# Prompt attention of a hybrid decoder layer: GpSimd in one fixed order, merge weights through DRAM in longer runs, two merged-block buffers, the first value loads on another queue

## The chip, the cores and the metric

The kernel runs on one core of a Trainium2 chip, with 16 DMA engines beside its compute engines. The metric is device time in microseconds (us) from one launch. The time before is 2846.34 us, the median of 3 runs (2836.22 to 2849.17).

## The reference, cut to what matters

One decoder layer over a prompt of 2048 tokens and 8 short samples. Of its parts only the prompt attention and the projection behind it matter here. Each of 8 heads (64 wide) attends in three dilated windows, and the three results are merged by their softmax denominators:

```
PATTERNS = ((128, 1), (512, 4), (2048, 16))
...
def combine_patterns(results):
    outs = jnp.stack([o for o, _ in results], axis=0)
    lses = jnp.stack([l for _, l in results], axis=0)
    w = jax.nn.softmax(lses, axis=0)
    return jnp.sum(w[..., None] * outs, axis=0)

def prompt_attn(q, k, v):
    return combine_patterns([dilated_prompt(q, k, v, w, d) for w, d in PATTERNS])
...
    mixed = jnp.concatenate([o_a.reshape(B, T, -1), o_b.reshape(B, T, -1)], axis=-1).astype(x.dtype) @ w_o
```

## The kernel before, in words

The program has three stages: projections and linear attention, then the prompt attention (`attention`), then the output projection and the feed-forward net (`tail`). The feed-forward net takes more than half of the span and is not touched.

**Attention.** Heads are worked on in four pairs (`pr` 0 to 3). A pair has three patterns (`pat`) of four groups (`g`) each: groups 0 to 3, 4 to 7 and 8 to 11. A group of patterns 0 and 1 has two units of work, one of pattern 2 has one, so a pair has 20 units. A unit (`AtUnit`) is: scores on TensorE (`pas`, L1787), mask and row minimum on VectorE and the exponential on ScalarE, transposes of the result on TensorE (`pat`, L1813), and products with the values (`pao`, L1830). The units are staggered: a unit's transposes come two units after its scores, its products three. TensorE's order over the units is fixed by hand (`AtUnit.line` chains each instruction to the one ahead of it).

**Gathers.** Patterns 1 and 2 need the queries regrouped. `at_gather` has GpSimd copy one tile per head (`aqg`, L1118), two per group, called at the first unit of the group two ahead. There are five such tiles, which is two and a half groups.

**Merge.** When a pair's last unit has been drained, which is three units into the next pair, `at_merge` starts as a generator that the loop advances once per group of patterns 0 and 1. It works out the three weights per head and row (L1130 to L1166), transposes them (`pab`), stores them to DRAM (`d_awd`, L1184, 48 KB) and loads them back spread over 64 rows per head (`awb`, L1173, two loads of 384 KB per block of 512 columns, each row in 12 runs of 512 bytes). For each of four blocks GpSimd then multiplies the three pattern outputs (`aop`) by the weights (L1211), adds them (L1215, L1217, into `amo`) and the block is stored (`d_mixa`, L1219). There are two `awb` tiles and one `amo` tile. The last pair has no next pair to hide behind: its weights are spread by TensorE transposes and multiplied on VectorE (L1209).

**Order.** The order on every engine but TensorE is made by a scheduler that plays a timeline of its own; it may put a merge step ahead of a gather that stands earlier in the code. DMA-issuing queues (SyncE and GpSimd) run strictly in the order so made. A queue that waits holds all that stands behind it.

**Loads.** `at_loadv` brings one group's values (`av`, four DMAs of 64 KB with 512-byte rows) two groups ahead, into six tiles. `at_load` brings queries and keys of a pair (`aqs`, `akh`, `akl`, in halves of 64 rows) from DRAM scratch; for the first pair they come in column pieces at the start.

**Projection.** `wo` needs eight inputs, each split in a high and a low part (`xh`, `xl`, L68 and L71): inputs 4 to 7 are the linear attention's, 0 to 3 the merged pairs', in the order `WORD = (4, 5, 6, 7, 0, 1, 2, 3)`. `wo_pre` prepares the first four during the last pair, `wo_x(0)` the others by loading `d_mixa` back.

Of the kernel before, what the change touches and what calls it, by code (L numbers as in the profile page):

```python
# [27 lines left out]
H = 264  # L28
# [8 lines left out]
class Layer:  # L37
# [918 lines left out]

    AB = dict(mw=1, qg=5, vsb=5, mq='p', klh=1, q=2, v=6, s=6, pt=5, op=5, ps=3, ppt=2, po=2, am=1, skew=(2, 3), man=(), ea=3, ed=5, mp=12, aa=(1, 4, 7, 9, 10), ms='ppps', mv=2, em=1)

# [24 lines left out]
    def attention(self):  # L983
        with ExitStack() as ctx:
# [36 lines left out]
            for _ in range(2):  # L1021
                p.tile([128, 3, 4, 128], F32, name=self.n("awb"), tag="awb", bufs=2)
            p.tile([128, 512], F32, name=self.n("amo"), tag="amo", bufs=1)
            pre = iter(())
            for pr in range(4):
# [6 lines left out]
                for pat in range(3):  # L1032
# [44 lines left out]
    def at_loadv(self, i):  # L1077
        nc = self.nc
        pr, pat, n = i // 12, i // 4 % 3, i % 4
        es = slice(128 * pr, 128 * pr + 128)  # L1080
        vo = self.a["o_vp"]
        t = self.aq[1].tile([128, 4, 128], F32, name=self.n("av"), tag="av", bufs=self.AB["v"])
        for j in range(4):
            if pat == 0:
                nc.sync.dma_start(t[:, j, :], vo.rearrange("(c r b i) e -> c b r i e", c=4, r=16, b=4)[n, j, :, :, es])
            elif pat == 1:
                nc.sync.dma_start(t[:, j, :], vo.rearrange("(c s r i) e -> r c s i e", c=4, s=4, r=4)[n, j, :, :, es])
            else:
                nc.sync.dma_start(t[32 * j:32 * j + 32],
                                  vo.rearrange("(c r i) e -> c i r e", c=4, r=16)[j, :, 4 * n:4 * n + 4, es])  # L1090
        self.vq += [t[:, j] for j in range(4)]

    def at_operands(self, qk, h, pat, g, blk):
# [17 lines left out]
        return lq, [cap(k, 32 * idx, [[512, 4], [1, 32]]) for k in K], [idx], idx  # L1111

    def at_gather(self, qk, pat, g):
        qg = []
        for h in range(2):
            t = self.ap.tile([128, 4, 128], F32R, name=self.n("aqg"), tag="aqg", bufs=self.AB["qg"])
            src = cap(qk[0][h], g, [[512, 4], [4, 128]]) if pat == 1 else cap(qk[0][h], 4 * g, [[1, 4], [16, 128]])
            self.nc.gpsimd.tensor_copy(t, src)  # L1118
            qg.append(t)
        self.qgn.append(qg)  # L1120

    def at_merge(self, pr, ML, OP):
# [30 lines left out]
        aw = p.tile([128, 3, 16, 2], F32, name=self.n("aaw"), tag="aaw", bufs=2)  # L1153
        for i in range(3):
            em.tensor_tensor(aw[:, i], ws[i][:, :, 0:2], mm, op=ALU.subtract)
        awf = aw.rearrange("p i b h -> p (i b h)")
        nc.scalar.activation(awf, awf, AF.Exp, scale=-1.0)
        dn = p.tile([128, 3, 16, 2], F32, name=self.n("adn"), tag="adn", bufs=1)
        for i in range(3):
            em.tensor_tensor(dn[:, i], aw[:, i], ws[i][:, :, 2:4], op=ALU.mult)  # L1160
        em.tensor_tensor(mm, dn[:, 0], dn[:, 1], op=ALU.add)
        em.tensor_tensor(mm, mm, dn[:, 2], op=ALU.add)
        mf = mm.rearrange("p b h -> p (b h)")
        nc.vector.reciprocal(mf, mf)
        for i in range(3):
            em.tensor_tensor(aw[:, i], aw[:, i], mm, op=ALU.mult)  # L1166
        last = pr == 3

        def weights(cb):
            W = p.tile([128, 3, 4, 128], F32, name=self.n("awb"), tag="awb", bufs=2)  # L1170
            if not last:
                for h in range(2):
                    nc.gpsimd.dma_start(W[64 * h:64 * h + 64],  # L1173
                                      bass.AP(tensor=wd.tensor, offset=wd.offset + 128 * h + 256 * cb,
                                              ap=[[0, 64], [4096, 3], [1024, 4], [1, 128]]))
            return W

        if not last:
            pt = pp.tile([128, 512], F32, name=self.n("pab"), tag="am", bufs=AB["am"])
            nc.tensor.transpose(pt[:96, :128], awf, self.ident)  # L1180
            wt = p.tile([128, 512], F32, name=self.n("awt"), tag="amo", bufs=1)[:96, :128]
# [8 lines left out]
        for cb in range(4):  # L1190
# [3 lines left out]
            else:  # L1194
                W, nxt = nxt, weights(cb + 1) if cb < 3 else None
            mo = p.tile([128, 512], F32, name=self.n("amo"), tag="amo", bufs=1)
            for i in range(3):
                if last:
                    tg = tags[j % 3]
                    pb = pp.tile([128, 4, 128], F32, name=self.n("pab"), tag=tg, bufs=AB[dict(am="am", ao="po")[tg]])  # L1200
                    ab = W[:, i].rearrange("p r (h e) -> p r h e", h=2)
                    src = cap(aw, i * 32 + 2 * cb, [[8, 4], [1, 2], [0, 64]])
                    if j in AB['aa']:
# [6 lines left out]
                else:  # L1210
                    (nc.gpsimd if j % 12 < AB["mp"] else nc.vector).tensor_tensor(  # L1211
                        OP[i][:, :, sl], OP[i][:, :, sl], W[:, i], op=ALU.mult)
                j += 1
            e = nc.vector if last else nc.gpsimd
            e.tensor_tensor(OP[0][:, :, sl], OP[0][:, :, sl], OP[1][:, :, sl], op=ALU.add)  # L1215
            e = nc.vector if last and cb >= AB["mv"] else nc.gpsimd
            e.tensor_tensor(mo.rearrange("p (m r) -> p r m", r=4),  # L1217
                            OP[0][:, :, sl], OP[2][:, :, sl], op=ALU.add)
            (dict(p=nc.gpsimd, s=nc.sync, a=nc.scalar)[AB['ms'][pr]]).dma_start(self.a["mixa"][:, pr, 512 * cb:512 * cb + 512],  # L1219
                                                       mo)  # L1220
            if cb < 3:
# [38 lines left out]

    pnmm = pbmm = atpe = None
    lastmm, gk = None, "g"
# [77 lines left out]
    def wo_pre(self):  # L1340
# [7 lines left out]
        yield  # L1348
        for k in self.WORD[:4]:
            hi, lo = self.hl()  # L1350
# [16 lines left out]
    def wo_x(self, c):  # L1367
# [615 lines left out]
```

## Time and profile before

| what | us |
|---|---|
| median of 3 runs | 2846.34 (2836.22 to 2849.17) |
| the profiled execution, its own time | 2844.27 |
| its span, first to last instruction | 2842.5 |
| TensorE busy, of the span | 2682.9 (94%) |
| VectorE, ScalarE, GpSimd busy | 1841.9, 1268.1, 602.3 |
| TensorE waiting on VectorE's `aop` copies, 750 to 1160 us | 22.8 (once) |
| TensorE waiting on GpSimd's gathers, same stretch | 21.8 (4 times) |

In the page the 40 slices show where TensorE is not at nine tenths: slices 11 to 17, about 710 to 1210 us, where attention lies. Its busy time there is to be read against idle time and what ended it, and the granted clock beside it: after an idle stretch the clock stands below 1.00. A busy share of GpSimd of 21% is an average over the span; in attention it is near half.

### The profile page before, as it was taken

What the parts mean: (1) busy time and instruction counts of PE and PEld (TensorE: products, weight loads), DVE (VectorE), ACT (ScalarE), POOL (GpSimd) and SP (SyncE); (2) the same over time, 40 slices, a digit from 0 to 9 for tenths busy, and PEclk for the clock granted to TensorE, in tenths of its full rate; (3) what the DMA queues carried; (4) which work ended last, traced back from release to release, by engine and by line L of the source; (5) the groups of instructions that cost most, each with busy time, mean ns of one, the idle gap of its engine ahead of it and who ended that gap; (6) DMA issues with size and microseconds to landing.
All of it is one profiled execution on the core that took longest, in us unless ns stands there. A gap on an engine that the chain in (4) does not pass through costs nothing. (4 is left out here: it accounts for less than half of the span.)

```text
span 2842.5 us, 58662 instructions
## 1 busy us (share of the span) xinstructions
PE 2682.9 (94%) x22255; PEld 2529.1 (89%) x22255; DVE 1841.9 (65%) x4557; ACT 1268.1 (45%) x2958; POOL 602.3 (21%) x751
## 2 busy tenths in 40 slices
PE   7999999999988967998899999999999999999997
PEld 6788899788877856998899999899999999999997
DVE  7667654443356746466889988676567766666666
ACT  6535433333267855344455545443334433443332
POOL 3424242443324557003110002000020000200001
PEclk9999999999989989999999999999999999999998
DMA  8755445898888745267488668787588875876654
GB/s 296 256 176 183 166 146 180 299 329 328 288 176 172 180 113 126 92 207 284 173 284 297 234 224 306 277 289 265 199 313 285 294 264 190 323 256 216 221 191 146
DMA packets 285657, 657.09 MB, mean 231 GB/s; under 512 B 31856, under 2 KB 82672, under 8 KB 283328
## 3 DMA queue, kind: packets, MB, share of 16 engines
q1 hardware_dynamic: 254880, 576.50, 60.5%
q0 software_dynamic: 13408, 44.99, 5.1%
q10 hardware_dynamic: 17088, 31.86, 3.0%
q8 instruction: 175, 2.87, 0.4%
q14 instruction: 106, 0.87, 0.1%
HBM read 509.29 MB, written 143.94 MB: 230 GB/s over the span
## 5 line engine op out<-in xcount | busy, mean ns | idle before, releaser
L68 ACT ACTIVATE ws<-wr 128x512 fp32r<-128x512 f32 (+1 forms) x482 | 293.0, 616 | 434.3 <-PE pfe L1559 135.6
L90 PE MATMUL pfd<-hh,ws 128*128 128x264 f32 x2816 | 475.5, 285 | 8.7 <-ACT ws L68 4.4
L90 PEld LDWEIGHTS pfd<-hh,ws 128*128 128x128 f32 x2816 | 399.5, 188 | 11.9 <-ACT ws L68 5.8
L71 DVE TENSOR_TENSOR ws<-wr,ws 128x512 fp32r<-128x512 f32 (+1 forms) x482 | 319.4, 668 | 140.0 <-ACT ws L68 136.4
L90 PE MATMUL pfd<-hl,ws 128*128 128x264 f32 x1408 | 303.0, 284 | 1.2 <-DVE hl L71 1.2
L1559 PE MATMUL pfa<-xh,ws 128*128 128x264 f32 x1496 | 293.2, 287 | 5.5 <-ACT ws L68 3.2
L1559 PE MATMUL pfe<-xh,ws 128*128 128x264 f32 x1496 | 289.9, 286 | 4.0 <-DMA ws<-d_wst 2.5
L1559 PE MATMUL pfd<-xh,ws 128*128 128x264 f32 x1408 | 289.2, 285 | 0.3 <-DVE gt L1546 0.2
L1559 PEld LDWEIGHTS pfa<-xh,ws 128*128 128x128 f32 x1496 | 237.4, 190 | 7.5 <-ACT ws L68 3.9
L1559 PEld LDWEIGHTS pfe<-xh,ws 128*128 128x128 f32 x1496 | 237.4, 190 | 4.6 <-DMA ws<-d_wst 2.7
L396 PE MATMUL pv<-wh,xh 128*128 128x256 f32 (+1 forms) x816 | 234.2, 287 | 1.1 <-DVE th L693 1.1
L1559 PEld LDWEIGHTS pfd<-xh,ws 128*128 128x128 f32 x1408 | 231.9, 189 | 0.7 <-DVE gt L1546 0.4
L396 PE MATMUL pv<-wl,xh 128*128 128x256 f32 (+1 forms) x816 | 231.8, 284 | 0.0
L396 PE MATMUL pv<-wh,xl 128*128 128x256 f32 (+1 forms) x816 | 231.0, 283 | 0.0
L90 PEld LDWEIGHTS pfd<-hl,ws 128*128 128x128 f32 x1408 | 225.3, 188 | 1.6 <-DVE hl L71 1.6
L1796 ACT ACTIVATE ass<-ass,aml 128x256 f32<-128x256 f32 (+1 forms) x384 | 173.6, 454 | 112.4 <-DVE aml L1792 86.8
L1508 POOL DMA_DIRECT2D xl<-d_xst x52 | 28.6, 551 | 892.4 <-PE pfe L1559 856.5
L1559 PE MATMUL pfd<-xl,ws 128*128 128x264 f32 x704 | 200.9, 285 | 0.0
L90 PE MATMUL pq<-xh,wh 128*128 128x512 f32 (+2 forms) x480 | 174.4, 371 | 10.2 <-ACT xh L234 7.8
L1559 PE MATMUL pfa<-xl,ws 128*128 128x264 f32 x616 | 176.7, 287 | 0.7 <-DMA xl<-d_xst 0.7
L1559 PE MATMUL pfe<-xl,ws 128*128 128x264 f32 x616 | 175.2, 285 | 0.0
L90 PE MATMUL pq<-xl,wh 128*128 128x512 f32 (+2 forms) x480 | 173.7, 363 | 0.0
(335 smaller groups left out, 6609.4 us busy)
## 6 DMA issues: line engine op xcount, KB each, us to landing
ws<-d_wst SPq DMA_DIRECT2D x248, 512.0 KB
wr<-in_wu SPq DMA_DIRECT2D x114, 512.0 KB
d_wst<-ws SPq DMA_DIRECT2D x88, 512.0 KB
wr<-in_wd SPq DMA_DIRECT2D x160, 256.0 KB
wr<-in_wt SPq DMA_DIRECT2D x60, 512.0 KB
wh<-d_wbs SPq DMA_DIRECT2D x35, 512.0 KB
wl<-d_wbs SPq DMA_DIRECT2D x35, 512.0 KB
skp<-in_ckt SPq DMA_DIRECT2D x16, 1024.0 KB
```

The lines of the kernel that those rows point to most:

```text
L68: h = nc.scalar.activation(hi, src, AF.Copy)
L71: return h, (nc.gpsimd if lo_eng == "p" else nc.vector).tensor_tensor(lo, src, hi.bitcast(F32), op=ALU.subtract)
L90: mm = nc.tensor.matmul(o, ww[:, k, :], xx[:, s0:s0 + n], start=(k == order[0] and i == 0), stop=(k == order[-1] and i == 2))
L396: mm = nc.tensor.matmul(ps[:m, :256], x[:, t0:t0 + m], w[:, k % 4, :], start=(k == 0 and i == 0), stop=(k == KT - 1 and i == 2))
L1508: self.nc.gpsimd.dma_start(t.bitcast(F32), xo[i, z])
L1559: self.lastmm = nc.tensor.matmul(bank[:, :H], w[:, ww, k, :], xx, start=new and k == 0 and j == 0, stop=k == 3 and j == 2, skip_group_chec ...
L1796: ex = nc.scalar.activation(ssb[:, sc:sc + nk], ssb[:, sc:sc + nk], AF.Exp, bias=self.ml[:, idx, h:h + 1], scale=-1.0, accum_out=self.ml[: ...
```

## The change

- **GpSimd's order.** A new helper `line` chains every gather, every merge instruction of pairs 0 to 2 and their DMA issues on GpSimd to the one ahead, so that GpSimd runs in the order of the code.
- **Merge weights.** The weight tile is laid out so that a block's weights for one head lie together: a load has one run of 6144 bytes per row in place of 12 of 512. One more `yield` stands between the store of the weights and the first load, so that the load comes a group later in the code.
- **Buffers.** `amo` has two tiles (one before); the transposed scores `apt` have four (five before).
- **Last pair.** Its weight arithmetic moves from VectorE to GpSimd (11 small operations). Its merged blocks use the six-tile ring `ass` in place of the single `amo`, are stored from GpSimd's queue in place of SyncE's, and the first two are split straight into input 3 of the projection, which is not loaded back. `wo_pre` prepares three inputs (4, 5, 6), and `wo_x(0)` the other four (7, 0, 1, 2).
- **Loads.** The values of the first two groups are issued by GpSimd in place of SyncE. The next pair's `at_load` is advanced in groups 5 to 10 in place of 0 to 7.

```
-                        if pat < 2:
+                        if 5 <= 4 * pat + g < 11:
                             self.qk0 = next(nxt, self.qk0)
...
     def at_loadv(self, i):
-        nc = self.nc
+        nc, e = self.nc, self.nc.gpsimd if i < 2 else self.nc.sync
...
+    def line(self, ins):
+
+        if self.atpo is not None:
+            self.after(ins, self.atpo)
+        self.atpo = ins
+        return ins
+
     def at_gather(self, qk, pat, g):
...
-            self.nc.gpsimd.tensor_copy(t, src)
+            self.line(self.nc.gpsimd.tensor_copy(t, src))
...
-            tm = p.tile([128, 512], F32, name=self.n("atm"), tag="amo", bufs=1)
+            tm = p.tile([128, 512], F32, name=self.n("atm"), tag="amo", bufs=2)
...
-        em = nc.vector if pr == 3 or not AB["em"] else nc.gpsimd
+        em, line = nc.gpsimd, (lambda x: x) if pr == 3 else self.line
...
-                    nc.gpsimd.dma_start(W[64 * h:64 * h + 64],
-                                      bass.AP(tensor=wd.tensor, offset=wd.offset + 128 * h + 256 * cb,
-                                              ap=[[0, 64], [4096, 3], [1024, 4], [1, 128]]))
+                    line(nc.gpsimd.dma_start(W[64 * h:64 * h + 64],
+                                           bass.AP(tensor=wd.tensor, offset=wd.offset + 1536 * (2 * cb + h),
+                                                   ap=[[0, 64], [512, 3], [128, 4], [1, 128]])))
...
-            nc.gpsimd.dma_start(wd, wt)
+            line(nc.gpsimd.dma_start(wd, wt))
+            yield
             nxt = weights(0)
...
+            if last:
+                mo = self.aq[1].tile([128, 512], F32, name=self.n("amo"), tag="ass", bufs=AB["s"])
...
+            if last and cb < 2:
+                if cb == 0:
+                    self.xnext[3] = self.hl()
+                o, m = ((0, 512), (512, 2 * H - 512))[cb]
+                self.split(*(t[:, o:o + m] for t in self.xnext[3]), mo[:, :m], "v")
...
-        for k in self.WORD[:4]:
+        for k in self.WORD[:3]:
...
-        for k in self.WORD[0 if c else 4:]:
+        for k in self.WORD if c else self.WORD[3:7]:
```

**GpSimd, the first merge (pair 0, worked off during pair 1), before.** The numbers behind the names are tiles. Blocks 0 and 1 are multiplied one after the other (`awb_10590`, `awb_10691`), then come the copies of a gather for group 6 and group 7, then the loads of blocks 2 and 3:

```order
L1211 TENSOR_TENSOR aop_9386<-aop_9386,awb_10691 128x4x128
L1211 TENSOR_TENSOR aop_9725<-aop_9725,awb_10691 128x4x128
L1211 TENSOR_TENSOR aop_10101<-aop_10101,awb_10691 128x4x128
L1215 TENSOR_TENSOR aop_9386<-aop_9386,aop_9725 128x4x128
L1118 COPY aqg_10821<-aqs_9721 128x512
L1118 COPY aqg_10927<-aqs_9444 128x512
L1173 DMA awb_10799<-d_awd 64x12x128 x2
L1215 TENSOR_TENSOR aop_9386<-aop_9386,aop_9725 128x4x128
L1173 DMA awb_10909<-d_awd 64x12x128 x2
L1217 TENSOR_TENSOR amo_10694<-aop_9386,aop_10101 128x4x128
```

And the same place of the changed kernel, from the gather of group 6 to that of group 7 (`aqg_10798` and `aqg_10800`, then `aqg_10903`):

```order
L1126 COPY aqg_10798<-aqs_9901 128x512
L1126 COPY aqg_10800<-aqs_10160 128x512
L1183 DMA awb_10888<-d_awd 64x1536 x2
L1225 TENSOR_TENSOR aop_9387<-aop_9387,awb_10781 128x4x128
L1225 TENSOR_TENSOR aop_9714<-aop_9714,awb_10781 128x4x128
L1225 TENSOR_TENSOR aop_10093<-aop_10093,awb_10781 128x4x128
L1228 TENSOR_TENSOR aop_9387<-aop_9387,aop_9714 128x4x128
L1230 TENSOR_TENSOR amo_10891<-aop_9387,aop_10093 128x4x128
L1232 DMA d_mixa<-amo_10891 128x512
L1126 COPY aqg_10903<-aqs_9901 128x512
```

Between two gathers there now stand always the two loads of the next block and one whole block; the gathers of groups 4 and 5 stand ahead of the first block, and the pattern repeats in pairs 1, 2 and 3.

**SyncE at the start of attention, before.** Pair 0's key pieces for columns 512 to 1023 end with `akl_9277`; `av_9349` and `av_9354` are the values of groups 0 and 1:

```order
L1073 DMA akh_9246<-d_kh_65 64x512 x2
L1085 DMA av_9349<-out_o_vp 128x1x128 x4
L1085 DMA av_9354<-out_o_vp 128x1x128 x4
L1073 DMA akl_9277<-d_kl_69 64x512 x2
L1085 DMA av_9387<-out_o_vp 128x1x128 x4
L1073 DMA aqs_9116<-d_qh_57 64x2x512
```

And in the changed kernel:

```order
L1074 DMA akh_9246<-d_kh_65 64x512 x2
L1074 DMA akl_9277<-d_kl_69 64x512 x2
L1086 DMA av_9388<-out_o_vp 128x1x128 x4
L1074 DMA aqs_9116<-d_qh_57 64x2x512
```

The eight value loads are gone from SyncE; on GpSimd they stand behind four of the stores of `out_o_vp`. Behind this place three groups' values now stand ahead of pair 1's loads; for pairs 2 and 3 SyncE's order of pair loads and values is as it was.

**VectorE at the end of the last merge, before.** `aop` are the last pair's outputs, `pab` the spread weights, `amo` blocks 2 and 3, `xl` the low parts of inputs 0 to 3:

```order
L1209 TENSOR_TENSOR aop_13432<-aop_13432,pab_13872 128x4x128
L1215 TENSOR_TENSOR aop_12575<-aop_12575,aop_13012 128x4x128
L1217 TENSOR_TENSOR amo_13831<-aop_12575,aop_13432 128x4x128
L1217 TENSOR_TENSOR amo_13857<-aop_12575,aop_13432 128x4x128
L71 TENSOR_TENSOR xl_13899<-br_13900,xh_13898 128x528
L71 TENSOR_TENSOR xl_13905<-br_13906,xh_13904 128x528
```

And in the changed kernel, where the first `xl` behind the blocks is input 7's:

```order
L1223 TENSOR_TENSOR aop_13427<-aop_13427,pab_13873 128x4x128
L1230 TENSOR_TENSOR amo_13832<-aop_12576,aop_13427 128x4x128
L1228 TENSOR_TENSOR aop_12576<-aop_12576,aop_13003 128x4x128
L1230 TENSOR_TENSOR amo_13858<-aop_12576,aop_13427 128x4x128
L1348 MEMSET halo 128x44
L71 TENSOR_TENSOR xl_13900<-br_13901,xh_13899 128x528
L71 TENSOR_TENSOR xl_13906<-br_13907,xh_13905 128x528
```

The order is nearly the same; the two block sums now write tiles of the ring of six, and two pieces of input 3's low part (`xl` from `amo`) stand a few rows earlier.

## Rows read from the trace of the kernel before

**Rows 1.** Stretches: busy us of each engine, clock, DMA share; pairs 1 to 3, the start.

```profile
857.70:939.80 82.10, 68.12 (x662) 60.25 (x660) 50.14 (x231) 55.89 (x219) 47.34 (x55) 0.90 0.85 175
939.80:1008.20 68.40, 65.87 (x661) 58.43 (x659) 50.66 (x231) 56.42 (x220) 33.37 (x42) 0.98 0.74 163
1008.20:1103.20 95.00, 65.10 (x621) 57.48 (x619) 50.86 (x218) 54.22 (x202) 56.61 (x66) 0.84 0.58 131
...
780.00:790.00 10.00, 4.91 (x28) 4.36 (x28) 4.32 (x24) 4.99 (x21) 0.54 (x1) 0.77 0.57 158
```

**Rows 2.** TensorE's waits, 750 to 1160 us: total, times, longest.

```profile
PE pao L1830 <- DVE aop L63: 22.8, 1, 22.8
PE pas L1787 <- POOL aqg L1118: 21.8, 4, 10.7
PE pbo L1405 <- DVE xl L71: 7.6, 1, 7.6
```

**Rows 3.** TensorE's timeline, pair 2: first scores of the pair, of groups 8 and 9.

```profile
939.78 0.33 PE L1787 MATMUL pas<-akh,aqs 128*128 128x128 f32 x1
...
988.85 0.33 PE L1787 MATMUL pas<-akh,aqg 128*128 128x128 f32 x1
...
992.49 0.33 PE L1787 MATMUL pas<-akh,aqg 128*128 128x128 f32 x1
```

**Rows 4.** GpSimd's groups of instructions: count, busy us, mean ns, idle before.

```profile
L1118 POOL CAST aqg<-aqs 128x512 fp32r<-128x512 f32 x64 | 68.5, 1099 | 58.4 <-PE pas L1787 38.5 <-DMA aqs<-d_ql 12.7 <-DMA aqs<-d_qh 5.8
L1211 POOL TENSOR_TENSOR aop<-aop,awb 128x512 f32<-128x512 f32 x36 | 44.6, 1269 | 34.3 <-DMA awb<-d_awd 34.3
...
L1217 POOL TENSOR_TENSOR amo<-aop,aop 128x512 f32<-128x512 f32 x14 | 18.6, 1325 | 21.7 <-DMA d_mixa<-amo 21.7
L1173 POOL DMA_DIRECT2D awb<-d_awd x24 | 18.0, 756 | 9.8 <-DMA d_awd<-awt 8.0 <-issue 1.7
...
L1215 POOL TENSOR_TENSOR aop<-aop,aop 128x512 f32<-128x512 f32 x12 | 15.2, 1273 | 0.1
...
L1219 POOL DMA_DIRECT2D d_mixa<-amo x12 | 6.9, 578 | 2.1 <-POOL amo L1217 1.8 <-DVE aaw L1166 0.3
```

**Rows 5.** GpSimd's timeline in pair 1: start, duration, then idle before and its releaser.

```profile
876.37 0.56 POOL L1184 DMA_DIRECT2D d_awd<-awt  x1 [2.61 <-DVE awt L63]
884.26 2.99 POOL L1173 DMA_DIRECT2D awb<-d_awd  x4 [7.34 <-DMA d_awd<-awt]
897.10 7.36 POOL L1211 TENSOR_TENSOR aop<-aop,awb 128x512 f32<-128x512 f32 x6 [9.84 <-DMA awb<-d_awd]
```

**Rows 6.** DMA issues, us to landing: windows 907, 1013, 1092 (`awb`), 870, 1060 (`awd`).

```profile
awb<-d_awd POOLq DMA_DIRECT2D x2, 384.0 KB, 9.5
...
awb<-d_awd POOLq DMA_DIRECT2D x2, 384.0 KB, 13.7
...
awb<-d_awd POOLq DMA_DIRECT2D x2, 384.0 KB, 7.6
...
d_awd<-awt POOLq DMA_DIRECT2D x1, 48.0 KB, 7.6
...
d_awd<-awt POOLq DMA_DIRECT2D x1, 48.0 KB, 3.1
```

**Rows 7.** SyncE's issues at the start of attention.

```profile
777.47 7.51 SPq L1085 DMA_DIRECT2D av<-out_o_vp  x8
785.03 1.24 SPq L1073 DMA_DIRECT2D akl<-d_kl  x2
...
795.48 1.25 SPq L1073 DMA_DIRECT2D akl<-d_kl  x2
```

**Rows 8.** TensorE's timeline there: the last score matmul that waits for such a load.

```profile
805.57 0.55 PE L1787 MATMUL pas<-akl,aqs 128*128 128x256 f32 x1 [1.75 <-DMA akl<-d_kl]
```

**Rows 9.** VectorE's timeline at the end of the last merge.

```profile
1132.24 0.68 DVE L1215 TENSOR_TENSOR aop<-aop,aop 128x512 f32<-128x512 f32 x1
1137.41 1.06 DVE L1217 TENSOR_TENSOR amo<-aop,aop 128x512 f32<-128x512 f32 x1 [4.50 <-DMA d_mixa<-amo]
1141.00 1.10 DVE L1217 TENSOR_TENSOR amo<-aop,aop 128x512 f32<-128x512 f32 x1 [2.53 <-DMA d_mixa<-amo]
1141.93 2.55 DVE L71 TENSOR_TENSOR xl<-br,xh 128x528 fp32r<-128x528 f32 x4
```

More of the change, by code (lines that the diff above doesn't have):

```diff
@@ L1022, in attention @@
                 p.tile([128, 3, 4, 128], F32, name=self.n("awb"), tag="awb", bufs=2)
-            p.tile([128, 512], F32, name=self.n("amo"), tag="amo", bufs=1)
+            for _ in range(2):
+                p.tile([128, 512], F32, name=self.n("amo"), tag="amo", bufs=2)
             pre = iter(())
@@ L1084, in at_loadv @@
             if pat == 0:
-                nc.sync.dma_start(t[:, j, :], vo.rearrange("(c r b i) e -> c b r i e", c=4, r=16, b=4)[n, j, :, :, es])
+                e.dma_start(t[:, j, :], vo.rearrange("(c r b i) e -> c b r i e", c=4, r=16, b=4)[n, j, :, :, es])
             elif pat == 1:
-                nc.sync.dma_start(t[:, j, :], vo.rearrange("(c s r i) e -> r c s i e", c=4, s=4, r=4)[n, j, :, :, es])
+                e.dma_start(t[:, j, :], vo.rearrange("(c s r i) e -> r c s i e", c=4, s=4, r=4)[n, j, :, :, es])
             else:
-                nc.sync.dma_start(t[32 * j:32 * j + 32],
+                e.dma_start(t[32 * j:32 * j + 32],
                                   vo.rearrange("(c r i) e -> c i r e", c=4, r=16)[j, :, 4 * n:4 * n + 4, es])
@@ L1152, in at_merge @@
         nc.vector.tensor_tensor(mm, mm, ws[2][:, :, 0:2], op=ALU.min)
-        aw = p.tile([128, 3, 16, 2], F32, name=self.n("aaw"), tag="aaw", bufs=2)
+        aw = p.tile([128, 96], F32, name=self.n("aaw"), tag="aaw", bufs=2)
+        at = lambda i: cap(aw, 4 * i, [[1, 4], [24, 4], [12, 2]])
+        rc = lambda t: t.rearrange("p (r c) h -> p r c h", r=4)
         for i in range(3):
-            em.tensor_tensor(aw[:, i], ws[i][:, :, 0:2], mm, op=ALU.subtract)
-        awf = aw.rearrange("p i b h -> p (i b h)")
+            line(em.tensor_tensor(at(i), rc(ws[i][:, :, 0:2]), rc(mm), op=ALU.subtract))
+        awf = aw
         nc.scalar.activation(awf, awf, AF.Exp, scale=-1.0)
@@ L1159, in at_merge @@
         for i in range(3):
-            em.tensor_tensor(dn[:, i], aw[:, i], ws[i][:, :, 2:4], op=ALU.mult)
-        em.tensor_tensor(mm, dn[:, 0], dn[:, 1], op=ALU.add)
-        em.tensor_tensor(mm, mm, dn[:, 2], op=ALU.add)
+            line(em.tensor_tensor(rc(dn[:, i]), at(i), rc(ws[i][:, :, 2:4]), op=ALU.mult))
+        line(em.tensor_tensor(mm, dn[:, 0], dn[:, 1], op=ALU.add))
+        line(em.tensor_tensor(mm, mm, dn[:, 2], op=ALU.add))
         mf = mm.rearrange("p b h -> p (b h)")
@@ L1165, in at_merge @@
         for i in range(3):
-            em.tensor_tensor(aw[:, i], aw[:, i], mm, op=ALU.mult)
+            line(em.tensor_tensor(at(i), at(i), rc(mm), op=ALU.mult))
         last = pr == 3
@@ L1180, in at_merge @@
             nc.tensor.transpose(pt[:96, :128], awf, self.ident)
-            wt = p.tile([128, 512], F32, name=self.n("awt"), tag="amo", bufs=1)[:96, :128]
+            wt = p.tile([128, 512], F32, name=self.n("awt"), tag="amo", bufs=2)[:96, :128]
             self.evac(wt, pt[:96, :128], "v")
             wd = self.a["awd"][pr]
-            nc.gpsimd.dma_start(wd, wt)
+            line(nc.gpsimd.dma_start(wd, wt))
+            yield
             nxt = weights(0)
@@ L1195, in at_merge @@
                 W, nxt = nxt, weights(cb + 1) if cb < 3 else None
-            mo = p.tile([128, 512], F32, name=self.n("amo"), tag="amo", bufs=1)
+            if last:
+                mo = self.aq[1].tile([128, 512], F32, name=self.n("amo"), tag="ass", bufs=AB["s"])
+            else:
+                mo = p.tile([128, 512], F32, name=self.n("amo"), tag="amo", bufs=2)
             for i in range(3):
@@ L1201, in at_merge @@
                     ab = W[:, i].rearrange("p r (h e) -> p r h e", h=2)
-                    src = cap(aw, i * 32 + 2 * cb, [[8, 4], [1, 2], [0, 64]])
+                    src = cap(aw, 24 * cb + 4 * i, [[1, 4], [12, 2], [0, 64]])
                     if j in AB['aa']:
@@ L1210, in at_merge @@
                 else:
-                    (nc.gpsimd if j % 12 < AB["mp"] else nc.vector).tensor_tensor(
-                        OP[i][:, :, sl], OP[i][:, :, sl], W[:, i], op=ALU.mult)
+                    line(nc.gpsimd.tensor_tensor(OP[i][:, :, sl], OP[i][:, :, sl], W[:, i], op=ALU.mult))
                 j += 1
[L1214 to L1220, printed above, removed]
+            e, le = (nc.vector, lambda x: x) if last else (nc.gpsimd, line)
+            le(e.tensor_tensor(OP[0][:, :, sl], OP[0][:, :, sl], OP[1][:, :, sl], op=ALU.add))
+            e, le = (nc.vector, lambda x: x) if last and cb >= AB["mv"] else (nc.gpsimd, line)
+            le(e.tensor_tensor(mo.rearrange("p (m r) -> p r m", r=4),
+                               OP[0][:, :, sl], OP[2][:, :, sl], op=ALU.add))
+            line(nc.gpsimd.dma_start(self.a["mixa"][:, pr, 512 * cb:512 * cb + 512], mo))
+            if last and cb < 2:
[3 more added lines that the diff above has]
+                self.split(*(t[:, o:o + m] for t in self.xnext[3]), mo[:, :m], "v")
             if cb < 3:
@@ L1259, in ssq_add @@
             return (nc.gpsimd if eng == "p" else nc.vector).tensor_tensor(ssq[:, :w], ssq[:, :w], sq[:, :w], op=ALU.add)
-    pnmm = pbmm = atpe = None
+    pnmm = pbmm = atpe = atpo = None
     lastmm, gk = None, "g"
```

2 lines of the change are left out of this document (1 added, 1 removed).

## The prediction

> **What bounds the kernel now.** I read the page's slices first, then the stretches, TensorE's waits, and the timelines of the engines that end them. The slices say that TensorE is at nine tenths nearly everywhere but in attention, so only what shortens TensorE's idle time there can count. The stretches [rows 1] give it by pair. Pair 1 lasts 82.1 us, pair 2 68.4, and pair 3 95.0 to its last group; TensorE is busy 68.1, 65.9 and 65.1 of that, and the granted clock is 0.90, 0.98 and 0.84. The reader is to see that the work is equal and the length is not. TensorE's waits [rows 2] name three causes: 22.8 us once for a copy into `aop`, 21.8 us in four waits for gathers, and 7.6 us for a low part in the projection. The first two are one matter, GpSimd: the `aop` tile is not free until the merge of an older pair is done.
>
> How long would a pair be without waits? Pair 2 runs to its group 9 almost undisturbed: from 939.78 to 992.49 is 52.7 us, and groups 8 to 9 are 3.65 us apart [rows 3]. A free pair is then 52.7 + 3 x 3.65 = 63.65 us. Against that pair 1 loses 18.4, pair 2 4.8 and pair 3, up to its last group (60.0), 35.0: together 58 us, clock losses behind the stalls included.
>
> **GpSimd's fixed order.** The order rows above show what becomes of a group: gather, two loads, one whole block. By GpSimd's means [rows 4] a block costs three multiplies (3 x 1.269), two sums (1.273 + 1.325) and the issue of its store (0.578), 7.0 us. A gather is two copies (2 x 1.099, 2.2 us), a pair of loads 2 x 0.756 = 1.5 us. A group of patterns 0 and 1 takes TensorE about 6.1 us (49.1 us for the eight [rows 3]), so GpSimd, at 10.7 us per group for two groups and 9.2 for the next, falls behind as soon as the first block starts, and the gathers are held behind the blocks. From the start of the first block to the first copy of group 9's gather there are four blocks, three gathers, two pairs of loads and one copy: 28.0 + 6.6 + 3.0 + 1.1 = 38.7 us. Groups 10 and 11 follow with no block between.
>
> If C is the time from the pair's first scores to the first block's first multiply, the pair stalls C + 38.7 - 52.7. Nothing in the change speeds the head of the merge: the weights' store is issued at 876.37, 18.7 us into pair 1, and landed before the loads of 884.26, at 26.6 us [rows 5]. Before, the first multiply came at 39.4 us [rows 5]. Now two loads are issued there in place of four, in runs of 6144 bytes. Two 512-byte-run loads landed 9.5 us after issue at a busy time, 13.7 at worst, 7.6 at a quiet one [rows 6]. No row has the long runs; a lower end is 3.1, the landing of the 48 KB store in a quiet stretch [rows 6], and the upper the 13.7. I take 7 for pairs 1 and 2, which lies nearer the 9.5, since the bytes are the same and only the pieces are fewer: C = 26.6 + 0.75 + 7 = 34.3, stall 20.3 each. In pair 3 no further pair is loaded; the store may land in 3.1 as it did there against 7.6 in pair 1 [rows 6], the loads are issued at about 22, and with 5.5 for their landing C = 28.3, stall 14.3. Sum 54.9, and 1.5 us per pair for the lower clock behind the last stall: 59 against 58. **The fixed order neither gains nor loses: -1 us.** The 22.8 us wait goes, because the old merge is done by group 7; in its place three gathers or four come late in every pair. Bounds: with C as small as GpSimd's own issues allow (31.8 and 27.2) the sum is 49 with no clock loss, a gain of 9; with landings of 13.7 it is 81, a loss of 23.
>
> **The start.** SyncE holds akl's issue behind eight value loads for 7.5 us, from 777.5 to 785.0, and the last of the column pieces goes out at 795.5 [rows 7]; TensorE waits for it until 805.6 [rows 8]. With the eight loads on GpSimd all these issues move up by at most 7.5 us. The DMA engines were 0.57 busy from 780 to 790 [rows 1], so 4.3 us of their time stood free there and must carry the same bytes. I take 5 us, between 4.3 and 7.5; the lower end is 0, if the landings set the pace of the queue. Covers: the values of group 0 are wanted behind three units' scores, so their 4 us on GpSimd's queue lie beside TensorE's waits. That three groups' values now go ahead of pair 1's loads costs nothing, since pair 1 begins 50 us later. For pairs 2 and 3 the loads do not move at all in SyncE's order: zero.
>
> **The end.** VectorE's last sum ends at 1132.9; then two block sums wait for the single `amo` to be stored, 4.50 and 2.53 us, and the low parts that TensorE needs come only at 1141.93 [rows 9]. This is the 7.6 us wait [rows 2]. With tiles of the ring the two sums (about 1.06 us each) follow at once, some 0.8 us of input 3's low part are added, and the first low part (input 7's, 0.64) is done near 1136.4 in place of 1142.6: 6.2 us sooner. Input 7's 6 matmuls no longer lie ahead of the wait (0.75 us lost); the shorter pause and 11 small operations fewer on VectorE are worth about 1.5. I take 7, between 3 (if the weights' arithmetic on GpSimd delays the head) and 10 (the waits of 7.0 plus all of the arithmetic and the clock).
>
> **Edits at nothing.** `apt` with four tiles: a unit's transposes follow on TensorE the products that free them, so the fifth tile was slack. The stores of the last blocks on GpSimd's queue: it is idle by then. Input 3 from SBUF: its load back lay behind the same `amo` wait.
>
> **Sum.** 5 + 7 - 1 = 11 us less than the profiled execution's own 2844.3, so 2833. That execution stands 2.1 us below the median, and the runs that will be compared are like the median: **2835**. Counted as no change is what lies within 0.5%, 14.2 us, about what a measurement of this kernel can tell: 2832.1 to 2860.6.
>
> **The rivals.**
>
> *The loads come early.* If the long runs land so fast that only GpSimd's own issues set C, the stalls are 49 and not 59; with 7.5 at the start and 10 at the end the sum is 26.5 to 27, 2820. For it: GpSimd waited 34.3 us for `awb` [rows 4], all of it with short pieces. Against it: the head and the weights' store are unchanged, and they make two thirds of C.
>
> *The long runs gain nothing.* Then C is 26.6 + 0.75 + 9.5 = 36.8 in pairs 1 and 2, and in pair 3 22 + 0.75 + 7.6 = 30.4; stalls 22.8, 22.8 and 16.4, with the clock 66.5, a loss of 8.5 in the middle. With 5 and 7 the sum is +3.5 us, 2843. For it: the bytes are the same, and the two loads of a block read one small piece of DRAM 64 times. [...]
>
> *Slower.* GpSimd's chain is now serial, and one late load holds gathers that before could pass it. If the loads land after 13.7 us [rows 6] in every pair, with the pair loads and values in their way, the stalls are 81 us, 23 more than now; with the start at 0 (the landings set the queue's pace) and 5 at the end that is +18, 2864. It decides where the first multiply stands beyond about 41 us into pairs 1 and 2. For it: landings of 13.7 were seen in pair 3, and the weights' store itself took 7.6. Against it: two loads are in flight in place of four at the first block.
>
> *The pair loads do not move.* For two of three pairs the order rows say so already; it is priced above at zero.
>
> **Numbers.** The forecast, a small gain, has 0.47; its own range is 2829 to 2842, and a quarter of it lies below 2832.1. The early loads have 0.26 (2820), long runs without gain 0.17 (2843), slower 0.10 (2864). Faster by over 0.5% is 0.26 + 0.12 = 0.38; within 0.5% 0.35 + 0.17 = 0.52; slower 0.10. The range leaves out the outer half of the slow case and the outer part of the early one: 2817 to 2853.
>
> **What would show it.** In the changed kernel: no wait of TensorE on `aop` above 3 us; some 10 to 14 waits of 3 to 6 us for gathers, for groups 6 to 9 of pairs 1 to 3, about 50 us in sum; the first multiply 34 us into pairs 1 and 2, 28 into pair 3; TensorE's last wait for a first-pair load ending near 800; the wait for `xl` below 2 us and VectorE without a wait on `d_mixa`. I am wrong if the gathers' waits sum to under 35 us (early loads) or above 70 (slower), or if pairs 1 to 3 come out even shorter than pair 2 was.

## The result, and the profile after

The changed kernel takes 2853.8 us at the median of 15 runs (2844.7 to 2864.2), the kernel before, on the same chip, 2845.0; the ratio is 1.0037, 95% interval 1.002 to 1.0053. By the bound of 0.5% that is no change; against the forecast of a gain it is a small loss, and it lies just above the range. The profiled execution after took 2848.22 us (span 2846.2), 3.95 more than the one before. The sums from the traces below account for this difference; the medians differ by 8.7 us, since the profiled execution lies 5.6 us under its median, and six of the 15 runs lie at 2861.6 and above with a lower mean clock (0.965 to 0.968, the others 0.969 to 0.974).

The stretches by pair, as in [rows 1], are the first thing to read. The work is the same, but TensorE is busy 77.0, 76.4 and 68.8 us where it was 68.1, 65.9 and 65.1, at a clock of 0.82 to 0.87.

```profile
851.30:943.70 92.40, 76.96 (x661) 68.30 (x659) 50.44 (x231) 56.17 (x219) 51.27 (x60) 0.83 0.80 174
943.70:1039.30 95.60, 76.44 (x662) 67.69 (x660) 50.40 (x231) 56.13 (x219) 51.27 (x60) 0.82 0.52 124
1039.30:1118.90 79.60, 68.78 (x621) 60.32 (x619) 54.12 (x217) 54.72 (x205) 53.74 (x60) 0.87 0.52 144
```

Against free pairs of 63.65, 63.65 and 60.0 us the three lose 28.8, 31.9 and 19.6, 80 us, where they lost 58. What is not busy is idle: 45.4 us in the three stretches, where it was 46.4. So TensorE does not wait longer than before in sum; the added 22 us lie in its busy time, which rose by 23.1 us. TensorE's waits, against [rows 2]:

```profile
PE pas L1804 <- POOL aqg L1126: 44.3, 16, 9.7
PE pas L1804 <- DMA akh<-d_kh: 3.8, 1, 3.8
...
PE pao L1847 <- DVE apt L63: 1.7, 2, 1.6
...
PE pbo L1422 <- DVE xl L71: 1.4, 1, 1.4
```

The wait for `aop` is gone, and sixteen for gathers stand in its place, as forecast. But they sum to 44.3 us, less than the loss of 80: nearly all of the rest is work that runs slowly. GpSimd's timeline in pair 1 shows the chain, against [rows 5]:

```profile
870.01 0.55 POOL L1194 DMA_DIRECT2D d_awd<-awt  x1 [2.20 <-DMA akh<-d_kh]
870.56 2.24 POOL L1126 CAST aqg<-aqs 128x512 fp32r<-128x512 f32 x2
874.56 1.06 POOL L1183 DMA_DIRECT2D awb<-d_awd  x2 [1.76 <-DMA d_awd<-awt]
...
887.81 3.71 POOL L1225 TENSOR_TENSOR aop<-aop,awb 128x512 f32<-128x512 f32 x3 [9.03 <-DMA awb<-d_awd]
891.49 1.25 POOL L1228 TENSOR_TENSOR aop<-aop,aop 128x512 f32<-128x512 f32 x1
892.82 1.28 POOL L1230 TENSOR_TENSOR amo<-aop,aop 128x512 f32<-128x512 f32 x1
894.40 0.61 POOL L1232 DMA_DIRECT2D d_mixa<-amo  x1 [0.30 <-POOL amo L1230]
895.00 2.12 POOL L1126 CAST aqg<-aqs 128x512 fp32r<-128x512 f32 x2
897.05 1.04 POOL L1183 DMA_DIRECT2D awb<-d_awd  x2
898.10 3.74 POOL L1225 TENSOR_TENSOR aop<-aop,awb 128x512 f32<-128x512 f32 x3
...
924.90 6.05 POOL L1126 CAST aqg<-aqs 128x512 fp32r<-128x512 f32 x6
```

From one block's first multiply to the next (887.81, 898.10) are 10.3 us, and TensorE's groups 6 to 8 follow at 10.3 us and group 9 at 9.2, each on its gather. Up to there slow work costs nothing, since the gather sets the time (the filled waits, below, leave group 9 where it was). After 924.90 the last three gathers are made at once, and nothing holds TensorE any more. What it does then is in these stretches:

```profile
920.00:926.00 6.00, 3.56 (x26) 2.94 (x25) 2.56 (x11) 2.54 (x14) 5.62 (x7) 0.72 0.44 129
926.00:932.00 6.00, 6.00 (x36) 5.51 (x36) 1.87 (x16) 4.18 (x18) 4.95 (x5) 0.56 0.20 56
932.00:939.00 7.00, 7.00 (x42) 6.50 (x40) 2.65 (x17) 3.85 (x18) 0.00 (x0) 0.50 1.05 232
939.00:944.00 5.00, 5.00 (x49) 4.33 (x45) 3.22 (x19) 2.54 (x13) 0.00 (x0) 0.86 0.62 140
```

It is busy without a pause, and the granted clock is 0.56 and 0.50. Groups 9 to 11, up to the next pair's first scores (in pair 3 up to the last group's), take 17.7 us here, 18.4 in pair 2 and 10.1 in pair 3. At 3.65 us per group [rows 3] that would be 10.95, 10.95 and 7.3; the kernel with free gathers, below, takes 11.35, 11.35 and 7.5 at a clock of 1.00.

The landings, against [rows 6]: the loads ahead of the first block in pairs 1, 2 and 3 (where there are four, the median), then the store in pairs 1 and 2.

```profile
awb<-d_awd POOLq DMA_DIRECT2D x4, 384.0 KB, 11.7
...
awb<-d_awd POOLq DMA_DIRECT2D x2, 384.0 KB, 11.3
...
awb<-d_awd POOLq DMA_DIRECT2D x4, 384.0 KB, 6.4
...
d_awd<-awt POOLq DMA_DIRECT2D x1, 48.0 KB, 4.3
...
d_awd<-awt POOLq DMA_DIRECT2D x1, 48.0 KB, 7.5
```

The start, against [rows 7] and [rows 8], SyncE's queue and then TensorE's last wait for a load of the first pair: `akl` is issued at 784.02 and 788.30 where it was 785.03 and 795.48, and the wait (which the profile puts down to a value load) ends at 798.3, not 805.6.

```profile
784.02 1.25 SPq L1074 DMA_DIRECT2D akl<-d_kl  x2
...
788.30 1.69 SPq L1074 DMA_DIRECT2D akl<-d_kl  x2
```

```profile
798.34 0.55 PE L1804 MATMUL pas<-akl,aqs 128*128 128x256 f32 x1 [1.72 <-DMA av<-out_o_vp]
```

The end, against [rows 9], VectorE: neither block sum waits for a store.

```profile
1146.82 1.10 DVE L1230 TENSOR_TENSOR amo<-aop,aop 128x512 f32<-128x512 f32 x1
1147.74 0.69 DVE L1228 TENSOR_TENSOR aop<-aop,aop 128x512 f32<-128x512 f32 x1
1148.47 1.07 DVE L1230 TENSOR_TENSOR amo<-aop,aop 128x512 f32<-128x512 f32 x1
1149.45 0.67 DVE L71 TENSOR_TENSOR xl<-br,xh 128x528 fp32r<-128x528 f32 x1
```

### The profile page after: what moved, and what is told of

Same layout as the page of the kernel before. It is cut to its first block, busy times and chain, and to the rows that moved or that the text cites. A ratio compares the mean times of both kernels' runs of the same rounds, so it can differ in the third digit from the quotient of the medians.

```text
span 2846.2 us, 58634 instructions
## 1 busy us (share of the span) xinstructions
PE 2700.3 (95%) x22255; PEld 2545.0 (89%) x22255; DVE 1843.6 (65%) x4547; ACT 1270.0 (45%) x2959; POOL 604.7 (21%) x774
## 5 line engine op out<-in xcount | busy, mean ns | idle before, releaser
L1809 DVE CUSTOM_DVE_ANT_0 ass<-pas,atab 128x256 f32<-128x256 f32 (+1 forms) x384 | 118.1, 361 | 114.9 <-PE pas L1804 99.8
```

Of the source, the lines that this page charges most:

```text
L1809: red = nc.vector.tensor_tensor_reduce(ssb[:, sc:sc + nk], ps[:, sc:sc + nk], L.amk[self.pat][:, 256 - nk:256], scale=1.0, scalar=3e38, op ...
```

## The experiments

Times are medians; ratios are to the kernel before on the same chip, with 95% intervals. "Loss" is the sum over pairs 1 to 3 of what is above a free pair, from TensorE's timeline of the one profiled execution (58 before, 80 after). From the 49th product of the projection to the end, behind all edits, the profiled executions take 1686 to 1701 us (1695.0 before, 1692.6 after), so a few us between two single executions show nothing.

### Taking the fixed order away, or adding it alone

The edit of the first is in `line`; the second puts the same chaining into the kernel before.

```diff
     def line(self, ins):
-        if self.atpo is not None:
-            self.after(ins, self.atpo)
-        self.atpo = ins
         return ins
```

> The changed kernel, but GpSimd's instructions are no longer chained: two merged-block buffers, long runs, the extra group before the reload, later pair loads, and the edits of the start and the end all stay. Theory (the fixed order is the loss, because gathers stand behind whole blocks): the stalls of pairs 1 to 3 fall from 80 us to between 50 and 65, as in the kernel before, while the start and the end keep what they gained (3.7 and 9.5 us): 2826 to 2838 us. Rival A (the long runs and the extra group, by which the first multiply comes 36.5 us into a pair, are the loss): the stalls stay at 75 to 85 and the time at 2848 to 2858. Rival B (start and end are given back behind attention): stalls as in the theory, the time 2840 to 2846.

**2815.8 us, 0.9905 (0.9876 to 0.9934).** Loss 50.5, the theory's lower end; pair 1 begins 74.5 us after attention's first score (77.9 before, 74.2 in the changed kernel), so the start keeps its gain. The time lies 10 us below the theory's lower end. Of this, 5.9 us in the profiled execution lie behind the 49th product (1689.1 for 1695.0); the runs with one part each, below, take up the rest.

> The kernel before with one thing of the change: GpSimd's gathers, merge loads, block work and stores chained in program order (four short-run loads and one merged-block buffer stay, no extra group). Theory: the middle loses what it lost in the changed kernel, 20 to 30 us, with many waits for gathers and a low clock behind the last of them, and nothing is gained at the start or the end: 2863 to 2876. Rival A (long runs, extra group and later loads are the loss): 2840 to 2852, the middle as before.

**2870.0 us, 1.0086 (1.0063 to 1.0109).** Loss 89.0, with 18 waits for gathers:

```profile
PE pas L1794 <- POOL aqg L1124: 59.2, 18, 10.2
```

Adding the order to one kernel costs 25 us, taking it from the other gives 38. Rival A, that the long runs or the later loads are the loss, falls with both. But one part of the expectation did not come: there is no low clock behind the last wait. Groups 9 to 11 of pairs 1 and 2 run at 0.98 and 1.00:

```profile
940.60:952.20 11.60, 11.60 (x119) 10.52 (x117) 8.22 (x52) 9.79 (x46) 1.09 (x1) 0.98 0.75 161
1033.10:1044.40 11.30, 11.30 (x118) 10.32 (x116) 8.35 (x53) 10.75 (x52) 3.28 (x4) 1.00 0.17 48
```

Here 87.5 of the 89.0 us are lost before group 9, where the first multiply stands 38.6, 37.9 and 32.7 us into the pairs.

### The long runs

```diff
-                                           bass.AP(tensor=wd.tensor, offset=wd.offset + 1536 * (2 * cb + h),
-                                                   ap=[[0, 64], [512, 3], [128, 4], [1, 128]])))
+                                           bass.AP(tensor=wd.tensor, offset=wd.offset + 128 * h + 256 * cb,
+                                                   ap=[[0, 64], [4096, 3], [1024, 4], [1, 128]])))
```

(and the weights' tile laid out as before)

> The changed kernel with the weights kept in their old layout, so that every reload is in runs of 512 bytes again. In the changed kernel the long-run loads landed after 11.7 and 11.3 us at the median in pairs 1 and 2, no faster than the short ones of the kernel before. Theory (the runs are worth nothing): landings 11 to 14 us, first multiply 36 to 39 us into pairs 1 and 2, the time within 4 us of the changed kernel, 2850 to 2858. Rival (long runs are what keeps the changed kernel from being slower still): landings 3 us or more longer, the first multiply beyond 40 us, 2860 to 2870.

**2854.9 us, 1.0032 (1.0016 to 1.0048)**, the same as the changed kernel. The loads ahead of the first block in pairs 1, 2 and 3, short runs:

```profile
awb<-d_awd POOLq DMA_DIRECT2D x4, 384.0 KB, 10.8
...
awb<-d_awd POOLq DMA_DIRECT2D x4, 384.0 KB, 10.6
...
awb<-d_awd POOLq DMA_DIRECT2D x4, 384.0 KB, 9.9
```

against 11.7, 11.3 and 6.4 with long ones. In pairs 1 and 2, where the next pair's loads are under way, the landing gains nothing. In pair 3, where no further pair is loaded, the long runs land 3.5 us sooner, and the first multiply stands 28.8 us into the pair and not 32.9. The long runs also save on the issue on GpSimd, 0.52 us each and not 0.76, so that groups follow at 10.3 us and not 10.8. That the times are equal all the same is a balance: with short runs pair 3 loses 24.9 us and not 19.6, but groups 9 to 11 of pairs 1 and 2 took 14.0 and 15.0 us in this execution and not 17.7 and 18.4.

### The start and the end alone

> The kernel before with the edits of the start (values of the first two groups loaded from GpSimd) and of the end (last pair's weights on GpSimd, merged blocks in the ring of score tiles, stores from GpSimd, input 3 from SBUF) alone; GpSimd's order of the middle, one merged-block buffer, short runs and the pair loads stay. Theory (the three terms add up, and only the middle was mis-sized): 3.7 us at the start and 9.5 at the end come through, 2829 to 2835. Rival B (what attention ends earlier is lost again behind it, or the end gains only because the middle was slow and the pair loads stood elsewhere): 2838 to 2846.

The edit leaves `at_loadv` and all `pr == 3` branches as in the changed kernel and sets the rest back. **2832.2 us, 0.9964 (0.9944 to 0.9985)**, 12 us less by the medians: the two terms come through, and Rival B falls. In the profiled execution the start gives 3.7 us and the end 7.8; the middle, which the edit leaves alone, loses 53.1 us and not 58, so a term read from two single executions is good to some 5 us.

### Which part gives the rest of the gain without the order

> The kernel with the edits of the start and the end (2832.2) plus the second merged-block buffer, the four `apt` tiles that make room for it, and the later pair loads; short runs, no extra group, no fixed order. It stands between that kernel and the changed kernel without the order (2815.8). Theory (the second buffer is what gives the 16 us, since a block's last sum no longer waits for the store of the block before, so that the `aop` tile is free earlier): 2812 to 2822, no wait of TensorE for `aop` over 5 us. Rival (the long runs and the extra group give them): 2828 to 2836, the wait for `aop` of 15 us and more still there.

> The kernel with the edits of the start and the end (2832.2) plus the long runs and the extra group between the weights' store and their reload; one merged-block buffer, five `apt` tiles, no fixed order. Theory (the second buffer gives the 16 us, long runs nothing): 2828 to 2838. Rival (the long runs and the extra group give them): 2812 to 2822.

**Two merged-block buffers: 2816.7 us, 0.9891 (0.9867 to 0.9915). Long runs and the extra group: 2820.1 us, 0.9915 (0.9893 to 0.9937).** The first time lies where its theory had it, but a wait of TensorE for `aop` of 9.1 us is left; the second goes its rival's way. So neither theory holds: either part alone gives 12 to 16 us on the 2832.2, and both together (2815.8) no more. In the second the wait for `aop` is 2.1 us. Both waits are from executions (2831.7 and 2828.9 us) that were the longest of six, so the median run may differ. Without the chain every such edit also lets the scheduler put GpSimd's instructions into another order, so that these runs do not say which wait each edit removes; that stays open.

### The order for the merge, not for the gathers

```diff
-            self.line(self.nc.gpsimd.tensor_copy(t, src))
+            self.nc.gpsimd.tensor_copy(t, src)
```

> The changed kernel with the fixed order kept for the merge (loads, block work, stores, each block whole and in turn) and lifted from the gathers alone. Theory (the loss of the fixed order is that gathers stand behind whole blocks, not that the merge is in order): the waits for gathers fall to under 25 us in sum, and the time to 2812 to 2828, near the changed kernel without any order (2815.8). Rival A (what costs is that the chain issues one block's loads late and so the merge ends late): waits for `aop` take the place of those for gathers, 2835 to 2850. Rival B (no effect, the gathers are late for another reason): 2848 to 2858.

**2809.2 us, 0.9877 (0.9856 to 0.9898)**, faster than both kernels and the best of all runs. Loss 41.9; TensorE's waits:

```profile
PE pas L1804 <- POOL aqg L1126: 13.4, 3, 7.6
PE pao L1847 <- DVE aop L63: 7.3, 2, 5.4
PE pas L1804 <- DVE aml L1809: 6.2, 2, 6.1
```

The blocks still follow each other. One line, by which gathers need not stand behind whole blocks, is worth 45 us by the medians; in the profiled executions 38 us of it lie in pairs 1 to 3.

### The clock behind the stalls

```diff
+        nf = {6: 16, 7: 10, 8: 10, 9: 10}.get(4 * self.pat + self.g, 0) if self.pr and self.u == 0 else 0
...
+            for _ in range(0 if h else nf):
+                self.line(nc.tensor.transpose(ps[:, :128], L.ident, L.ident))
```

> The changed kernel with TensorE given something to do in the waits: ahead of the scores of group 6 of pairs 1 to 3 it transposes the identity 16 times, ahead of those of groups 7, 8 and 9 10 times (about 0.28 us each, into the bank that the scores overwrite). This adds work and takes none away. In the changed kernel groups 9 to 11 of pairs 1 and 2, whose gathers were done, took 17.7 and 18.4 us up to the next pair's first scores at a granted clock near 0.50, where at full clock they take 11.2. Theory (the lower clock behind the stalls is the term that I mis-sized, and it comes from the pauses): the stalls of groups 6 to 9 stay as long as GpSimd makes them, groups 9 to 11 fall to about 11.2 us in each pair, 12 to 17 us less in all: 2836 to 2844. Rival A (the lower clock has another cause, or returns elsewhere): 2850 to 2856. Rival B (the fills are themselves too long, or delay the gathers' release): 2856 to 2865.

**2839.2 us, 0.998 (0.9965 to 0.9995)**: 138 matmuls more, and 14.6 us less than the changed kernel. Group 9 of pairs 1 to 3 begins 74.9, 75.7 and 69.0 us into its pair, where it was 74.7, 77.2 and 69.5: GpSimd's chain is as it was. Groups 9 to 11 take 14.4, 13.0 and 9.2 us in place of 17.7, 18.4 and 10.1, 9.6 us less in sum; the theory had them at full clock. (In the profiled executions another 5.0 us lie behind the 49th product, where nothing was edited.) Two of the fills, and the stretches behind the last wait of pair 1:

```profile
906.54 1.31 PE L1799 MATMUL pas<-c_ident 128*128 128x128 f32 x10
908.54 0.33 PE L1807 MATMUL pas<-akh,aqg 128*128 128x128 f32 x1 [0.69 <-POOL aqg L1126]
...
914.75 1.31 PE L1799 MATMUL pas<-c_ident 128*128 128x128 f32 x10
918.86 0.33 PE L1807 MATMUL pas<-akh,aqg 128*128 128x128 f32 x1 [2.80 <-POOL aqg L1126]
```

```profile
928.00:932.00 4.00, 3.94 (x19) 3.94 (x20) 1.16 (x11) 1.54 (x8) 4.00 (x6) 0.50 0.19 68
932.00:939.00 7.00, 7.00 (x62) 6.09 (x61) 3.41 (x26) 5.34 (x24) 0.99 (x1) 0.81 0.82 175
939.00:943.00 4.00, 4.00 (x43) 3.66 (x43) 3.20 (x19) 3.82 (x21) 0.00 (x0) 1.00 1.06 216
```

The clock is 0.81 from 932 to 939 and 1.00 behind it, where the changed kernel had 0.50 and 0.86. The fills of 1.3 us (2.8 expected) cost nothing: behind both TensorE still waits for its gather, 0.69 and 2.80 us. So more than half of the slow work behind the last wait came from the pauses, in this kernel. How long it lasts does not follow from the length of a pause alone: behind a wait of 4.87 us the kernel without the order ran at 0.50 for 19 us (last section), behind one of 22.8 us the kernel before for 4.

### The chain, shortened

The third multiply of each block of pairs 0 to 2 is left out, so that the third pattern goes into the sum unweighted.

```diff
-                    line(nc.gpsimd.tensor_tensor(OP[i][:, :, sl], OP[i][:, :, sl], W[:, i], op=ALU.mult))
+                    if i < 2:
+                        line(nc.gpsimd.tensor_tensor(OP[i][:, :, sl], OP[i][:, :, sl], W[:, i], op=ALU.mult))
```

> The changed kernel with GpSimd's third multiply of every merge block of pairs 0 to 2 left out (the third pattern enters the sum unweighted), nothing else: a probe of the chain. Theory (from the first multiply to group 9's gather the time is GpSimd's serial work, so a stall is the first multiply's place plus that chain minus TensorE's 52.7 us): four multiplies of 1.24 us fall out of the chain of 38.2 us, groups 7 to 9 follow at 9.1 us in place of 10.3, the stall of each pair is 5.0 us shorter, three pairs 15 us, and 0 to 5 us of the low clock with it: 2834 to 2841. Rival (loads or landings pace the blocks, and GpSimd's work lies beside them): the groups stay at 10 us and more and the time at 2846 to 2855.

**2833.2 us, 0.9961 (0.9945 to 0.9977)**, 20.6 less than the changed kernel and just below the forecast. Group 9 begins 71.0, 71.9 and 64.8 us into the pairs: 3.7, 5.3 and 4.7 sooner, 13.7 for 15 forecast. From the first multiply to group 9 are 34.1, 33.8 and 36.0 us, 4.1 to 4.6 less than with the third multiply. Groups 6 to 8 follow at 9.2 to 9.8 us. Groups 9 to 11 take 14.4, 13.0 and 10.4, so that some of the slow work went too. The rival falls.

### Moving work to VectorE

On the kernel with free gathers: `nc.vector` for `i == 2` in the block multiply (first), `em = nc.vector` for pairs 0 to 2 (second), both (third).

> The kernel with the merge in order and the gathers free (2809.2) and the third multiply of every merge block of pairs 0 to 2 moved to VectorE, which was busy 0.54 of the stretch: a candidate. Theory (GpSimd's work per pair still sets the end of the merge, and with it the waits for `aop` and gathers): GpSimd is relieved of 5 us per pair, 4 to 12 us less in all, 2797 to 2805. Rival (VectorE stands in its queue for the weights' landing with the scores' reductions behind it, and TensorE waits for `aml` or `ass` instead): 2812 to 2825.

> The kernel with the merge in order and the gathers free (2809.2) with the 11 small operations on the weights (0.25 us each on GpSimd, 128 x 32) moved to VectorE, so that the head of a merge has no hop between the two engines and no place in GpSimd's queue behind the older merge: a candidate, and a test of what the head is worth. Theory: the weights' store goes out 2 to 4 us sooner after a pair's start, the first multiply with it, and the stall of each pair is shorter by that: 2798 to 2807. Rival (the store's and the loads' landings vary by more than that, or VectorE's 2 us more per pair delay the reductions): 2807 to 2815.

> Both moves to VectorE at once, the third multiplies and the small operations, on the kernel with the merge in order and the gathers free (2809.2). Theory (they add): 2790 to 2802. Rival (VectorE becomes what TensorE waits for): slower than the better one of the two alone, 2805 to 2820.

**2827.5 us, 0.9934 (0.991 to 0.9957); 2812.3, 0.9889 (0.9867 to 0.9911); 2827.2, 0.9936 (0.9914 to 0.9958).** Each goes the rival's way, the first and third beyond its range. In the first VectorE, whose queue also holds the scores' reductions, stands waiting for the weights, and TensorE waits for VectorE (for `aml` 23.4 us, where the kernel it starts from has 6.2); the rows are VectorE's waits and then TensorE's:

```profile
DVE aop L1225 <- DMA awb<-d_awd: 44.1, 9, 12.0
```

```profile
PE pas L1804 <- DVE aml L1809: 23.4, 5, 9.0
```

In the third, too, TensorE's three largest waits are for VectorE (14.2, 13.7 and 11.0 us).

The second is the same as the kernel it starts from, but it does not test what a faster head is worth, because the head got slower. The weights' store goes out 22.4, 27.8 and 17.8 us into the pairs, where the kernel with free gathers has 18.7, 20.7 and 16.4: on VectorE the small operations stand between the scores' reductions. The stores of pair 1, which begins at 852.40 and at 853.42, small operations on VectorE first:

```profile
874.80 0.53 POOL L1195 DMA_DIRECT2D d_awd<-awt  x1 [22.80 <-DVE awt L63]
```

```profile
872.09 0.55 POOL L1194 DMA_DIRECT2D d_awd<-awt  x1 [2.19 <-DVE awt L63]
```

## Why the prediction was wrong

**The mechanism held.** The `aop` wait went, gathers came late in every pair, and a pair's stall is the first multiply's place plus GpSimd's chain minus 52.7 us. The chain was taken as 38.7 us; it is 38.2 (887.81 to group 9's first score at 926.00) in pair 1, 38.2 in pair 2, 40.7 in pair 3, and it shortens with GpSimd's own work, as the run without the third multiply shows. Most signs that the prediction named came true: no wait for `aop`, 44.3 us of waits for gathers for "about 50", the first pair's load at 798.3, the wait for `xl` at 1.4. They look at idle time, and the loss is in busy time; only the first multiply, below, missed its place.

**The step that failed first is "1.5 us per pair for the lower clock behind the last stall".** That is 4.5 us in sum; it is 17.0: 6.8, 7.4 and 2.8 (16.0 against the times at full clock that the kernel with free gathers shows). I took it from the kernel before, where the one long wait for `aop` was followed by full clock within some 4 us (it ends at 1036.91; 0.50 up to 1041, 0.83 up to 1042, then 1.00). In the changed kernel the clock stayed low for up to 15 us of work behind the last wait (in pair 1 0.59 from 926 to 930, 0.50 up to 940, 0.90 up to 942). The filled waits show that it is this term: with the chain unchanged, 9.6 us of it came back. Why it lasted so long stays open. The number of pauses does not decide it: with the order alone there were as many (18 waits for 16), and the work behind the last of them ran at 0.98 and 1.00 in pairs 1 and 2. Nor is it the same each time: with short runs and much the same pauses (15 waits, 48.4 us) the term was 10.9 us.

**The second is "I take 7 for pairs 1 and 2", the loads' landing.** It was 11.7 and 11.3 us, beyond the 9.5 of the row that I had called nearest. The first multiply came 36.5, 39.1 and 28.8 us into the pairs, where I had 34.3, 34.3 and 28.3; in pair 1 the earlier issue (23.3 us in, not 26.6) paid part of it back, in pair 2 the store took 7.5 to land. In pair 3 the 6.4 us were near the 5.5 taken. That is 7.5 us, and with the chain the stalls are 63.3 and not 54.9.

So the middle lost 80.3 - 58.3 = 22 us where I had 1. **The other terms were near.** The start gave 3.7 us (pair 1 begins 74.2 us after attention's first score, not 77.9), for 5. The end gave 9.5 (from the last group's first score to the projection's 49th product, when both kernels have the waits for low parts behind them, are 34.8 us, not 44.2), for 7. Part of that need not be the edit's: with the order alone and no edit of the end the same stretch took 37.7 us, and VectorE's two sums waited 0 and 2.14 us for a store where before they waited 4.50 and 2.53, so those waits differ from kernel to kernel. The sum is 22.1 - 3.7 - 9.5 = +8.9; attention also began 2.7 us earlier and all behind the 49th product took 2.4 less, which makes the spans' difference of 3.8. These are parts of one timeline and must add up to it; the 5 us by which the medians differ more are not located.

Of the rivals, the long runs that gain nothing had the first multiply about right in pairs 1 and 2 (36.5 and 39.1 for 36.8) and too late in pair 3 (28.8 for 30.4). Like the forecast it had too small a clock term; with 17.0 in place of 4.5 it would have stood at 2855. The chances put on it, 0.17, were too few, since the rows showed no load of that size at a busy time under 9.5 us.

## What to carry to other kernels

When one engine serves both a stream that another engine waits for every few microseconds and long background work, as GpSimd does here, fix the order of the background work alone and leave the stream free to pass it; tying both into one chain cost 25 to 45 us here. Price repeated short pauses of TensorE at their length plus slow work behind the last of them, and give that term a range: here it went from nothing to 7.4 us per pair in the kernels with the order, and the kernel before, where at most 5.5 us behind a wait ran at 0.50 (1090.48 to 1096), did not show its upper end. Fill the pause if it can't be removed. And look at busy time too: the idle time was near the forecast. Before moving work to a less busy engine, ask whether what that work waits for comes before the engine's other work is due; moving the third multiplies cost 18 us here.

## What the runs showed of the hardware

In the kernel without the order TensorE ran at a clock of 0.50 from 924 to 943, 19 us, and again from 1000 to 1013, 13 us, and was busy all the time:

```profile
924.00:932.00 8.00, 8.00 (x44) 7.34 (x44) 1.96 (x16) 3.93 (x17) 8.00 (x9) 0.50 0.71 174
932.00:943.00 11.00, 11.00 (x66) 9.68 (x64) 4.90 (x28) 6.38 (x28) 5.75 (x7) 0.50 0.88 196
1000.00:1013.00 13.00, 13.00 (x70) 11.68 (x68) 4.74 (x35) 7.66 (x35) 13.00 (x14) 0.50 0.36 82
```

In the kernel with free gathers, groups 9 to 11 behind a stall took 11.35 us in pairs 1 and 2, at a clock of 1.00. What decides between the two was not tried. And a 384 KB load that reads 6 KB of DRAM 64 times took 7.6 to 13.7 us to land in pieces of 512 bytes [rows 6], 6.4 to 11.7 in pieces of 6144 (medians of two or four loads). In the changed kernel and the one with short runs, which differ in the weights' layout alone, the longer pieces landed sooner ahead of the first block of pair 3 (6.4 for 9.9) and not of pairs 1 and 2; what else sets the time between these ends no run tells.
